# Six of eight output blocks transposed by VectorE and by transfers within SBUF, and the gate row summed in float32r

## The chip, the cores and the metric

The kernel runs on one core of one Trainium2 chip. A core has five engines that run side by side: TensorE (PE in the profile, with its weight loads apart as PEld), VectorE (DVE), ScalarE (ACT), GpSimd (POOL) and SyncE (SP, which here only issues transfers). The metric is the device time of one execution in microseconds (us), the median of several runs; less is better.

## The reference

One decoder layer: an adaLN-modulated RMSNorm, gated linear attention in chunks, a gated output projection and a final RMSNorm, on 1024 positions of width 1024, all in float32. Cut to what matters here:

```
mod = silu(c) @ ada_w + ada_b                      # shift, scale, gate: 1024 each
h   = rmsnorm(x, norm_g) * (1 + scale) + shift
q, k, v, g_lr, r = split(h @ w_in)
o   = gla(q, k, v, g_lr)                           # 4 heads, 1024 positions x 1024 values
o   = rmsnorm(o, gla_norm_g) * silu(r)
x   = x + gate * (o @ w_out)
out = rmsnorm(x, final_g)
```

Two parts of it are touched: `o` must be transposed so that its values lie on the partitions before `o @ w_out`, and `gate`, a row of 1024 sums, must stand on all 128 partitions before it is multiplied into `w_out`.

## The kernel before

The kernel does a float32 product as three float32r products: each operand is split into a high part (ScalarE copies it to float32r) and a low part (VectorE or GpSimd subtracts the high part), and `PAIRS` multiplies high with high, high with low and low with high. So each operand of a product passes through ScalarE and VectorE once.

The program is written in the order of PE's work, but issued in another: the class `Program` records every operation, and `schedule` plays them through with a table of costs (`cost`, `LAT`), in which each engine takes, of its operations that are ready, the one with the earliest latest start. What comes out is one fixed order for each engine; on the chip every engine works off its own list strictly in that order and waits at an instruction whose inputs aren't there. SP's transfers are issued from one such list too; each takes one of eight completion counters in turn, so that it waits for the transfer eight places ahead of it to have landed.

The main part is 32 steps `s`, 8 for each of four heads (`b = s // 8`) and one for each tile of 128 positions (`t = s % 8`). In a step PE forms the projection to v and r of one tile (24 products of 512 columns), and between them the hooks of `hooks(s)` run the linear attention of chunk `n = s - 4`: `e_head` to `e_kt` make the decays, `gla_at`, `gla_kv` and `gla_o` the products, and `gla_og` writes the gated, normed output of a chunk into `OG[n // 4]`, a tile of 128 positions by 4 by 256 values. So eight tiles `OG[b]` (b from 0 to 7) are filled one after the other, each over four steps. All of this goes through VectorE's list.

Then come 16 steps of the output projection, eight tiles for each half of the columns. `o_tr(t)` transposes the eight 128x128 blocks of one tile of positions on PE against the identity, into the PSUM banks `tr` and `md`, and splits them into `OT[t]` (tiles `hh` and `hl`), one step ahead of their use. `finish` adds the residual and takes the squares.

The gate row: `gate_acc` sums 16 pieces of `ada_w` times `silu(c)` into `GB` on VectorE, partition by partition, and `gate_bc(i)` adds up the 128 partitions of one half with a float32 product against a tile of ones on PE, whose result VectorE copies back into `GB`. `scale_piece` multiplies it into pieces of `w_out`.

In the trace the tile names stand without numbers: `ptr` and `pmd` are the PSUM banks `tr` and `md`, `ident` the identity, `qk` and `wa` the tiles that hold `OG` among others, `wg` is `GB`, `hh` and `hl` the split halves, `Sf` the attention state, `raw` pieces of a weight. Every operation is issued at one line, L217, so that rows are told apart by their tiles.

Of the kernel before, what the change touches and what calls it, by code (L numbers as in the profile page):

```python
# [8 lines left out]
F32R = mybir.dt.float32r  # L9
U8 = mybir.dt.uint8  # L10
AF = mybir.ActivationFunctionType
ALU = mybir.AluOpType
# [13 lines left out]
class Program:  # L26
# [7 lines left out]
    P = {"off": 8.0, "pad": 3.0}  # L34
# [29 lines left out]
    def cost(self, e, m, out, ins, kw):  # L64
        n = 1
        for d in out.shape[1:]:
            n *= d
        psum = any(a.space == bass.MemoryType.PSUM for a in ins + [out])
        if m == "dma_start":
            return n * out.shape[0] * 4 / 360e3  # L70
        if e == "pe":
            if m == "transpose":
                return 0.11
            k = 1 if ins[0].dtype == F32R else 4
            return 0.0135 + n * k / 2400 if n > 1 else 0.22
        if e == "act":
            return (0.05 if psum else 0.09) + n / 1200 + (0.2 if "accum_out" in kw else 0) + \
                (0.095 * sum(hasattr(kw.get(a, 0), "tensor") for a in ("scale", "bias")))
        if e == "dve":
            fast = m in ("tensor_copy", "tensor_scalar", "memset") and not psum  # L80
            return (0.13 if "scalar" in m else 0.068) + n * (0.52 if fast else 1.042) / 1000
        if m != "tensor_tensor":
            return 0.08 + n * 0.8 / 1000
        return 0.46 if kw.get("op") == ALU.pow else 0.11 + n * 2.1 / 1000
# [144 lines left out]
def gla_block(ctx, tc, x, c, ada_w, ada_b, norm_g, w_in, w_alpha, b_alpha, gn_g, w_out, final_g, out):  # L229
    nc = tc.nc  # L230
    prog = Program(nc)
    pe, act, dve, pool, sync = (prog.engine(e) for e in ("pe", "act", "dve", "pool", "sync"))
# [5 lines left out]
    def T(tag, shape, dt=F32):  # L238
        cnt[0] += 1
        return prog.tile(sb, tag, shape, dt, f"{tag}_{cnt[0]}")  # L240

    def P(tag, shape=(128, 512)):
        cnt[0] += 1
        return prog.tile(ps, "p" + tag, list(shape), F32, f"p{tag}_{cnt[0]}")

    def f(ap):
        return ap.bitcast(F32)
# [47 lines left out]
    ident = T("ident", [128, 128])  # L295
# [3 lines left out]
    ones = T("ones", [128, 128])  # L299
# [113 lines left out]
    def w_split(kt, c0=0, c1=384):  # L413
        if c0 == 0:
            WH[kt] = T(f"wa{2 * kt}", [128, D], F32R)
            WL[kt] = T(f"wa{2 * kt + 1}", [128, D], F32R)
        raw = WRAW[kt] if c0 == 0 else WRAW[kt, 3]
        hi, lo = (w[kt].rearrange("p (i c) -> p i c", i=2)[:, :, c0:c1] for w in (WH, WL))
        i = act.activation(hi, raw, AF.Copy)
        if c0 == 0 and kt > 1:  # L420
            prog.hold(i, HT[kt - 1])
        return dve.tensor_tensor(lo, raw, f(hi), op=ALU.subtract)
# [29 lines left out]
    def gate_w_load():  # L452
# [5 lines left out]
        for q0 in (0, 32, 96):  # L458
            sync.dma_start(war[q0:q0 + 16, :], w_alpha[0])

    def gate_w_conv():
        war = W["a"]
        act.activation(WA, war, AF.Copy)
        dve.tensor_tensor(WA[32:64, :], war[32:64, :], f(WA[32:64, :]), op=ALU.subtract)
# [46 lines left out]
    for kt in range(8):  # L511
# [5 lines left out]
        if kt == 0:  # L517
            for half in range(2):
                if half:
# [3 lines left out]
                    lo = w_split(1)  # L523
# [32 lines left out]
    gate_w_load()  # L556
    small_cols2()
    gate_w_conv()
    prog.first_loads = False
    for i, m in enumerate(M6):  # L560
# [25 lines left out]
    for i, m in enumerate((3, 7)):  # L586
        p = P(f"m{i}")
# [97 lines left out]
    OG, X, SHL, KD = {}, {}, {}, {}  # L685
# [128 lines left out]
    def og_tag(b):  # L814
        return f"wa{12 + b}" if b < 2 else f"qk{b // 2 - 1}{1 - b % 2}"
# [17 lines left out]
    GB = T("wg", [128, D])  # L833
# [11 lines left out]
    def gate_acc(i):  # L845
        kk, j = i // 2, i % 2
        g = GB[:, 512 * j:512 * j + 512]
        dve.scalar_tensor_tensor(g, GA[i], cact[:, kk:kk + 1], g, op0=ALU.mult, op1=ALU.add)

    def gate_bc(i):  # L850
        p = P("tr")
        pe.matmul(p, ones, GB[:, 512 * i:512 * i + 512], start=True, stop=True)
        dve.tensor_copy(GB[:, 512 * i:512 * i + 512], p)


    OT = {}

    def o_tr(t):
        oh = T(f"hh{t}", [128, 8, 128], F32R)
        ol = T(f"hl{t}", [128, 8, 128], F32R)  # L860
        OT[t] = (oh, ol)
        for g in range(2):
            p = P(("tr", "md")[g])
            for i in range(4):
                e = 4 * g + i
                src = OG[(e // 2) * 2 + t // 4][:, t % 4, 128 * (e % 2):128 * (e % 2) + 128]
                pe.transpose(p[:, 128 * i:128 * i + 128], src, ident)
            hi = oh[:, 4 * g:4 * g + 4, :].rearrange("p a b -> p (a b)")
            lo = ol[:, 4 * g:4 * g + 4, :].rearrange("p a b -> p (a b)")
            act.activation(hi, p, AF.Copy)  # L870
            dve.tensor_tensor(lo, p, f(hi), op=ALU.subtract)

    XRT = ["qk31", "G", "qk30", "wa7", "wa4", "wa5", "wa14", "wa8"]
    XR, FS = {}, {}
# [6 lines left out]
    def hooks(s):  # L881
        H = {}

        def at(k, fn, *a):
            H.setdefault(k, []).append((fn, a))

        n = s - LAG
        u = (s - 2) // 2
        b, t = s // 8, s % 8
        if t == 0 and 1 <= b < 6:  # L890
            for k in (6, 7):
                at(k - 6, conv_piece, b, k)
        if s % 4 == 1 and 5 <= s <= 33:
            at(4 if s < 33 else 0, silu, s // 4 - 1)
        if 0 <= u < 16:
            d = 0 if u > 3 else 2
            if s % 2 == 0:
                if d:
                    at(0, g_tr, u)
                at(d, e_head, u)  # L900
                at(3 + d // 2, e_scan, u)
                at(4 + d // 2, e_exp, u)
                at(6 + d // 2, e_mul, u)
            else:
                at(d // 2, e_split, u)
                at(3 + d // 2, e_kt, u)

        if 0 <= n - 1 < 32:
            at(0, gla_o, n - 1)
            at(6, gla_og, n - 1)  # L910
        if 0 <= n < 32:
            at(2, gla_at, n)
            at(5, gla_kv, n)
        if b < 5:
            x45, x67 = (f"qk{b}1", "wa6") if b < 4 else ("wa10", "wa11")
            if t == (2 if b >= 3 else 5):
                for k in range(4):
                    at(5, load_piece, b + 1, k)
            if (b, t) == (4, 4) or b < 4 and t == (2 if b == 3 else 5):
                for k in (6, 7):  # L920
                    at(5 if b < 4 else 0, load_piece, b + 1, k, x67)
            if t == 6:
                for k in (4, 5):
                    at(0, load_piece, b + 1, k, x45)
            if t == 7:
                for k in range(6):
                    at(k + 2, conv_piece, b + 1, k)
            if b >= 3:
                if 3 <= t < 6:
                    at(2, scale_piece, b + 1, (0, 2, 6)[t - 3])  # L930
                    at(5, scale_piece, b + 1, (1, 3, 7)[t - 3])
                if t == 6:
                    at(5, scale_piece, b + 1, 4)
                if t == 7:
                    at(0, scale_piece, b + 1, 5)
        if s < 5:
            for i in range(4):
                if s > 0:
                    at(i, gate_acc, 4 * (s - 1) + i)
                if s < 4:  # L940
                    at(4, gate_load, 4 * s + i)
            if s == 0:
                at(0, gate_init)
        if s == 5:
            at(0, gate_bc, 0)
        if s == 7:
            at(0, gate_bc, 1)
        if s >= 31 and s < 39:
            at(4 if s == 31 else 1, o_tr, s - 31)
        if s >= 32 and s < 40:  # L950
            at(4, load_xr, s - 32)
        return H
# [5 lines left out]
    for s in range(32):  # L958
        H = hooks(s)
        t = s % 8  # L960
        p = P(VB[s % 2])
# [6 lines left out]
        for kt in range(8):  # L968
            w = WP[s // 8, kt] if s >= 8 else WG[kt]
            for o, c0, c1 in groups:  # L970
                for j, (hi, wi) in enumerate(PAIRS):
                    h = (HH, HL)[hi][kt]
                    pe.matmul(o, h[:, 128 * t:128 * t + 128], w[:, wi, c0:c1],
                              start=(kt == 0 and j == 0), stop=(kt == 7 and j == 2))
# [7 lines left out]
    fg = None  # L982
    for s in range(32, 48):
        H = hooks(s)
        a, t = (s - 32) // 8, s % 8
        if a == 0:
# [8 lines left out]
        for i, (c0, c1) in enumerate(parts):  # L995
            p = P(VB[s % 2] if s < 47 else ("m0", "m1")[i])[:, 0:c1 - c0]
            for kt in range(8):
                w = WP[4 + a, kt]
                mm_o = OT[t]
                for j, (oi, wi) in enumerate(PAIRS):  # L1000
                    pe.matmul(p, mm_o[oi][:, kt, :], w[:, wi, c0:c1],
                              start=(kt == 0 and j == 0), stop=(kt == 7 and j == 2))
# [15 lines left out]
        if a == 1:  # L1018
            r = fss[:, 3:4]
# [32 lines left out]
```

## Time and profile before

| what | value |
|---|---|
| median of 3 runs | 453.7 us (453.37 to 455.35) |
| the profiled execution, its own time | 455.46 us |
| its span, first to last instruction | 453.7 us |
| PE busy | 440.6 us (97%) |
| VectorE busy | 313.4 us (69%) |
| ScalarE busy | 245.9 us (54%) |
| GpSimd busy | 127.8 us (28%) |
| granted clock, mean | 0.995 |

The profile is one execution on the chip. Busy is the time in which an engine had an instruction in work; matmuls are pipelined, so a matmul's own duration is longer than the distance to the next one, and it is the distance that counts for PE. An idle time is put down to what ended it. The chain of waits follows back from the last instruction what released each piece of work.

### The profile page before, as it was taken

Reading aid. Unit: us, or ns where it says so; the run is one execution under the profiler, and the core shown is the slowest. Engines: PE = TensorE matmul, PEld = TensorE weight load, DVE = VectorE, ACT = ScalarE, POOL = GpSimd, SP = SyncE. Lnnn points to the kernel's source line nnn. Section 1 sums busy time; section 2 is a strip of 40 time slices with the busy share of each in tenths; the row PEclk is TensorE's granted clock in tenths of the full one; section 3 lists DMA queues with packets and bytes.
Section 4 is the critical chain, followed back from the end, with each engine's and each line's share of the span. In section 5 each row is a group of like instructions: output and inputs, shape, how many; then the busy total and the mean of one; then the engine's idle time right before and its main releaser. Section 6 shows DMA issues by size and latency. Waiting matters only on the chain.

```text
span 453.7 us, 6865 instructions
## 1 busy us (share of the span) xinstructions
PE 440.6 (97%) x2426; PEld 377.8 (83%) x2426; DVE 313.4 (69%) x704; ACT 245.9 (54%) x564; POOL 127.8 (28%) x147
## 2 busy tenths in 40 slices
PE   8799999999999999999999999999999999999994
PEld 8687778888999998888888888878888888888883
DVE  2698856165216889987797877998789976464433
ACT  4675869110136667658668486685859641351111
POOL 3100201020002326442373524726256420040001
PEclk9999999999999999999999999999999999999998
DMA  8999752068200103100140001300014525002222
GB/s 270 351 310 305 249 119 60 25 189 266 56 1 0 48 12 93 38 0 12 36 117 24 0 12 36 117 24 1 1 47 147 190 95 172 1 1 92 92 94 92
DMA packets 40063, 43.09 MB, mean 95 GB/s; under 512 B 3847, under 2 KB 32685, under 8 KB 40030
## 3 DMA queue, kind: packets, MB, share of 16 engines
q1 hardware_dynamic: 39982, 42.65, 29.9%
q8 instruction: 19, 0.31, 0.3%
q14 instruction: 14, 0.11, 0.1%
q10 hardware_dynamic: 48, 0.01, 0.0%
HBM read 38.46 MB, written 4.19 MB: 94 GB/s over the span
## 4 chain that ended last, share of the span: by engine, by line
PE 73%; DVE 13%; DMA 6%; ACT 3%; issue 3%; SPq 1%; POOL 0%; POOLq 0%; DVEq 0%; ACTq 0%
PE pm L217 65%; DVE wa L217 7%; PE pmd L217 5%; DMA qk<-in_ada_w 4%; PE ptr L217 3%; DVE Sf L217 2%; DMA raw<-in_gla_w_in 1%; SPq L217 1%; ACT wa L217 1%; DVE x L217 1%; DVE v L217 1%; DVE raw L217 1%; DVE ATf L217 1%; ACT hl L217 0%; DVE rs L217 0%
## 5 line engine op out<-in xcount | busy, mean ns | idle before, releaser
L217 PE MATMUL pm<-x,hh 128*128 128x512 f32 (+2 forms) x424 | 121.9, 370 | 0.0
L217 PE MATMUL pm<-wa,hh 128*128 128x512 f32 (+2 forms) x424 | 120.6, 368 | 0.0
L217 PEld LDWEIGHTS pm<-wa,hh 128*128 128x128 f32 x424 | 73.5, 188 | 10.5
L217 PEld LDWEIGHTS pm<-x,hh 128*128 128x128 f32 x424 | 71.8, 189 | 9.0 <-issue 1.0
L217 PE MATMUL pm<-wa,hl 128*128 128x512 f32 (+2 forms) x212 | 77.3, 365 | 0.0
L217 PE MATMUL pm<-x,hl 128*128 128x512 f32 (+2 forms) x212 | 77.1, 364 | 0.0
L217 ACT ACTIVATE wa<-wa 128x256 f32<-128x256 f32 (+4 forms) x126 | 59.7, 496 | 21.6 <-DVE wa L217 16.4
L217 PE MATMUL pm<-hh,wa 128*128 128x512 f32 (+1 forms) x236 | 62.1, 386 | 1.0 <-ACT hh L217 1.0
L217 PEld LDWEIGHTS pm<-hh,wa 128*128 128x128 f32 x236 | 41.7, 188 | 9.2 <-ACT hh L217 2.0
L217 POOL TENSOR_TENSOR wa<-wa,wa 128x896 fp32r<-128x896 f32 (+1 forms) x22 | 43.0, 1956 | 14.0 <-ACT wa L217 14.0
L217 PEld LDWEIGHTS pm<-wa,hl 128*128 128x128 f32 x212 | 39.8, 188 | 6.7
L217 PEld LDWEIGHTS pm<-x,hl 128*128 128x128 f32 x212 | 39.8, 188 | 6.3
L217 PE MATMUL pm<-wa,wa 128*128 128x256 f32 (+1 forms) x208 | 38.5, 281 | 0.1
L217 POOL TENSOR_TENSOR Shl<-Sf,Shl 128x256 fp32r<-128x256 f32 x28 | 23.0, 821 | 47.4 <-ACT Shl L217 47.4
L217 PEld LDWEIGHTS pm<-wa,wa 128*128 128x128 f32 x208 | 31.7, 189 | 4.6 <-DVE wa L217 1.1
L217 POOL TENSOR_TENSOR ors<-oss,mh 128x1 f32<-128x1 f32 x32 | 19.7, 615 | 52.0 <-DVE oss L217 52.0
L217 ACT ACTIVATE qk<-pm 128x256 f32<-128x256 f32 (+1 forms) x31 | 12.9, 424 | 39.3 <-PE pm L217 30.7
L217 PE MATMUL pm<-hl,wa 128*128 128x512 f32 (+1 forms) x118 | 32.9, 382 | 0.0
L217 DVE TENSOR_TENSOR wa<-pm,wa 128x256 fp32r<-128x256 f32 (+2 forms) x37 | 17.9, 483 | 17.7 <-PE pm L217 11.3
L217 DVE TENSOR_TENSOR wa<-wa 128x256 f32<-128x256 f32 (+1 forms) x48 | 24.1, 525 | 8.1 <-ACT wa L217 7.9
L217 POOL TENSOR_TENSOR D<-wa 128x256 f32<-128x256 f32 x16 | 11.7, 732 | 62.5 <-DVE wa L217 58.8
L217 ACT ACTIVATE pm<-wa 128x512 f32<-128x512 f32 (+1 forms) x11 | 6.2, 561 | 38.1 <-DVE wa L217 30.9
(175 smaller groups left out, 766.7 us busy)
## 6 DMA issues: line engine op xcount, KB each, us to landing
qk<-in_ada_w SPq DMA_DIRECT2D x32, 256.0 KB, 5.8
raw<-in_gla_w_in SPq DMA_DIRECT2D x48, 128.0 KB, 2.2
raw<-in_ada_w SPq DMA_DIRECT2D x16, 256.0 KB, 3.4
raw<-in_gla_w_in SPq DMA_DIRECT2D x8, 384.0 KB, 5.7
qk<-in_x SPq DMA_DIRECT2D x6, 512.0 KB, 5.2
wa<-in_x SPq DMA_DIRECT2D x5, 512.0 KB, 4.1
x<-in_x SPq DMA_DIRECT2D x4, 512.0 KB, 3.4
raw<-in_gla_w_out SPq DMA_DIRECT2D x8, 256.0 KB, 3.7
```

The costliest lines, as they stand in the source:

```text
L217: getattr(self.eng[o["e"]], o["m"])(*o["call"][0], **o["call"][1])
```

## The change

Of the eight blocks `OG[b]`, those with b from 0 to 5 (heads 0 to 2) no longer go through PE. `o_blocks(b)`, hooked in the step in which such a block gets full, has VectorE transpose it in squares of 32 by 32 (four instructions of 128x256) into a tile `oy`, of which there is one, and SP move the 16 groups of squares within SBUF to where they belong, by 16 transfers of 32 partitions with 8 runs of 128 bytes each, into `O2[b]`. `o_tr(t)` then transposes only the two blocks of head 3 on PE, into one bank, and splits four pieces of 256 columns, three of them out of `O2` in SBUF, where it split two of 512 columns out of PSUM.

`gate_bc` multiplies with ones in float32r: `gate_split` first splits a half of `GB` into high and low on ScalarE and GpSimd, into the tile `wa6`, and PE does two float32r products where it did one float32 product. The tile of ones in float32r is one more VectorE instruction at the start. The table of costs gets a slower rate for transfers whose source is in SBUF. The order of all engines is worked out anew by the same rules.

```
--- before.py
+++ after.py
@@ -67,7 +67,7 @@
             n *= d
         psum = any(a.space == bass.MemoryType.PSUM for a in ins + [out])
         if m == "dma_start":
-            return n * out.shape[0] * 4 / 360e3
+            return n * out.shape[0] * 4 / (76e3 if ins[0].tensor.name in self.acc else 360e3)
         if e == "pe":
             if m == "transpose":
                 return 0.11
@@ -458,7 +458,10 @@
         for q0 in (0, 32, 96):
             sync.dma_start(war[q0:q0 + 16, :], w_alpha[0])
 
+    onesr = T("onesr", [128, 128], F32R)
+
     def gate_w_conv():
+        dve.tensor_copy(onesr, ones)
         war = W["a"]
         act.activation(WA, war, AF.Copy)
         dve.tensor_tensor(WA[32:64, :], war[32:64, :], f(WA[32:64, :]), op=ALU.subtract)
@@ -847,28 +850,51 @@
         g = GB[:, 512 * j:512 * j + 512]
         dve.scalar_tensor_tensor(g, GA[i], cact[:, kk:kk + 1], g, op0=ALU.mult, op1=ALU.add)
 
+    GS = {}
+
+    def gate_split(i):
+        if i == 0:
+            GS[0] = T("wa6", [128, 2, 512], F32R)
+        g = GB[:, 512 * i:512 * i + 512]
+        act.activation(GS[0][:, 0, :], g, AF.Copy)
+        pool.tensor_tensor(GS[0][:, 1, :], g, f(GS[0][:, 0, :]), op=ALU.subtract)
+
     def gate_bc(i):
         p = P("tr")
-        pe.matmul(p, ones, GB[:, 512 * i:512 * i + 512], start=True, stop=True)
+        for j in range(2):
+            pe.matmul(p, onesr, GS[0][:, j, :], start=j == 0, stop=j == 1)
         dve.tensor_copy(GB[:, 512 * i:512 * i + 512], p)
 
 
     OT = {}
+
+    def o_blocks(b):
+
+        y = T("oy", [128, 4, 8, 32])
+        for i in range(4):
+            dve.transpose(y[:, i].rearrange("p e i -> p (e i)"), OG[b][:, i, :])
+        O2[b] = T(og_tag(b), [128, 4, 2, 128])
+        yv = y.rearrange("p t (g c) i -> p t g c i", c=4)
+        for c in range(4):
+            for r in range(4):
+                sync.dma_start(O2[b][32 * c:32 * c + 32, :, :, 32 * r:32 * r + 32],
+                               yv[32 * r:32 * r + 32, :, :, c, :])
+
+    O2 = {}
 
     def o_tr(t):
         oh = T(f"hh{t}", [128, 8, 128], F32R)
         ol = T(f"hl{t}", [128, 8, 128], F32R)
         OT[t] = (oh, ol)
-        for g in range(2):
-            p = P(("tr", "md")[g])
-            for i in range(4):
-                e = 4 * g + i
-                src = OG[(e // 2) * 2 + t // 4][:, t % 4, 128 * (e % 2):128 * (e % 2) + 128]
-                pe.transpose(p[:, 128 * i:128 * i + 128], src, ident)
-            hi = oh[:, 4 * g:4 * g + 4, :].rearrange("p a b -> p (a b)")
-            lo = ol[:, 4 * g:4 * g + 4, :].rearrange("p a b -> p (a b)")
-            act.activation(hi, p, AF.Copy)
-            dve.tensor_tensor(lo, p, f(hi), op=ALU.subtract)
+        p = P(("tr", "md")[t % 2])
+        for i in range(2):
+            pe.transpose(p[:, 128 * i:128 * i + 128], OG[6 + t // 4][:, t % 4, 128 * i:128 * i + 128], ident)
+        for g in range(4):
+            hi = oh[:, 2 * g:2 * g + 2, :].rearrange("p a b -> p (a b)")
+            lo = ol[:, 2 * g:2 * g + 2, :].rearrange("p a b -> p (a b)")
+            src = O2[2 * g + t // 4][:, t % 4].rearrange("p a b -> p (a b)") if g < 3 else p[:, 0:256]
+            act.activation(hi, src, AF.Copy)
+            dve.tensor_tensor(lo, src, f(hi), op=ALU.subtract)
 
     XRT = ["qk31", "G", "qk30", "wa7", "wa4", "wa5", "wa14", "wa8"]
     XR, FS = {}, {}
@@ -941,10 +967,14 @@
                     at(4, gate_load, 4 * s + i)
             if s == 0:
                 at(0, gate_init)
+        if s == 4:
+            at(4, gate_split, 0)
         if s == 5:
             at(0, gate_bc, 0)
-        if s == 7:
-            at(0, gate_bc, 1)
+            at(0, gate_split, 1)
+            at(4, gate_bc, 1)
+        if s % 4 == 0 and 8 <= s <= 28:
+            at(7, o_blocks, s // 4 - 2)
         if s >= 31 and s < 39:
             at(4 if s == 31 else 1, o_tr, s - 31)
         if s >= 32 and s < 40:
```

What this moves is shown at three places. First PE's list in the output projection's first half, where a tile of positions is transposed between the products of a step; before:

```order
L217 MATMUL pm_545_608<-x_491_554,hh_532_595 128x512 x2
L217 MATMUL pm_545_608<-x_491_554,hl_533_596 128x512
L217 MATMUL ptr_612<-ident_72,wa_261_324 128x128 x2
L217 MATMUL ptr_612<-ident_72,qk_334_397 128x128 x2
L217 MATMUL pmd_613<-ident_72,qk_400_463 128x128 x2
L217 MATMUL pmd_613<-ident_72,qk_471_534 128x128 x2
L217 MATMUL pm_545_608<-x_492_555,hh_532_595 128x512 x2
```

and with the change, at the same place of the program:

```order
L217 MATMUL pm_555_618<-x_505_568,hh_543_606 128x512 x2
L217 MATMUL pm_555_618<-x_505_568,hl_544_607 128x512
L217 MATMUL ptr_622<-ident_72,qk_485_548 128x128 x2
L217 MATMUL pm_555_618<-x_506_569,hh_543_606 128x512 x2
L217 MATMUL pm_555_618<-x_506_569,hl_544_607 128x512
```

Four rows of two transposes became one row of two; the products around them stand as they did.

Second, VectorE's list around the first square transposes of block 2 (`oy`), in the second head's steps; before:

```order
L217 SCALAR_TENSOR_TENSOR qk_309_372<-pm_336_399,ors_285,qk_309_372 128x256
L217 SCALAR_TENSOR_TENSOR Sf_218_281<-Sf_219_282,dec_283,pm_339_402 128x256
L217 TENSOR_TENSOR wa_216_279<-pm_335_398,wa_216_279 128x256
L217 TENSOR_SCALAR wa_208_271<-ptr_410,cols_20_83 128x256
L217 TENSOR_SCALAR oss_284<-oss_284 128x1
L217 TENSOR_TENSOR wa_208_271<-wa_208_271 128x256
L217 COPY_PREDICATED ATf_206_269<-mask_267,pm_350_413 64x128
```

and with the change:

```order
L217 SCALAR_TENSOR_TENSOR qk_313_376<-pm_342_405,ors_286,qk_313_376 128x256
L217 SCALAR_TENSOR_TENSOR Sf_219_282<-Sf_220_283,dec_284,pm_345_408 128x256
L217 TENSOR_TENSOR wa_217_280<-pm_341_404,wa_217_280 128x256
L217 TENSOR_SCALAR wa_209_272<-ptr_416,cols_20_83 128x256
L217 TENSOR_SCALAR oss_285<-oss_285 128x1
L217 STREAM_TRANSPOSE oy_444<-qk_313_376 128x256
L217 TENSOR_TENSOR wa_209_272<-wa_209_272 128x256
L217 COPY_PREDICATED ATf_207_270<-mask_268,pm_356_419 64x128
```

The transpose into `oy` stands between the instructions of one chunk's output and those of the next unit's decays, and waits there until the 16 transfers of block 1 have read `oy`. The last transpose of block 1 stands 22 rows ahead of it:

```order
L217 SCALAR_TENSOR_TENSOR wa_263_326<-pm_333_396,ors_286,wa_263_326 128x256
L217 COPY Sf_220_283<-pm_336_399 128x256
L217 STREAM_TRANSPOSE oy_401<-wa_263_326 128x256
L217 TENSOR_TENSOR wa_209_272<-wa_209_272 128x256
L217 SCALAR_TENSOR_TENSOR wa_209_272<-rs_267,wa_209_272 128x256
```

Third, SP's list from the second head's weights on; before:

```order
L217 DMA raw_342_405<-in_gla_w_in 128x256 x2
L217 DMA raw_344_407<-in_gla_w_in 128x256 x2
L217 DMA wa_345_408<-in_gla_w_in 128x256 x4
L217 DMA qk_349_412<-in_gla_w_in 128x256 x4
L217 DMA raw_407_470<-in_gla_w_in 128x256 x2
L217 DMA raw_408_471<-in_gla_w_in 128x256 x2
L217 DMA raw_409_472<-in_gla_w_in 128x256 x2
```

and with the change:

```order
L217 DMA raw_349_412<-in_gla_w_in 128x256 x2
L217 DMA raw_350_413<-in_gla_w_in 128x256 x2
L217 DMA wa_351_414<-in_gla_w_in 128x256 x4
L217 DMA wa_312_375<-oy_374 32x8x32 x16
L217 DMA wa_339_402<-oy_401 32x8x32 x16
L217 DMA qk_355_418<-in_gla_w_in 128x256 x4
L217 DMA raw_417_480<-in_gla_w_in 128x256 x2
L217 DMA raw_418_481<-in_gla_w_in 128x256 x2
L217 DMA raw_419_482<-in_gla_w_in 128x256 x2
```

The 32 transfers of blocks 0 and 1 stand between the weights of one head and those of the next, and the weights behind them wait for VectorE's last transpose of block 1.

## Rows read from the trace of the kernel before

**Rows 1.** The page's busy times: us, share of the span, instructions.

```profile
PE 440.6 (97%) x2426; PEld 377.8 (83%) x2426; DVE 313.4 (69%) x704; ACT 245.9 (54%) x564; POOL 127.8 (28%) x147
```

**Rows 2.** What PE waited for, whole span: us in total, times, longest.

```profile
PE pmd L217 <- DVE D L217: 0.4, 1, 0.4
PE ptr L217 <- DVE wa L217: 0.3, 1, 0.3
```

**Rows 3.** Stretches: length; PE, PEld, DVE, ACT, POOL busy (count); clock; DMA share, GB/s.

```profile
146.00:176.00 30.00, 29.57 (x227) 27.47 (x226) 25.56 (x57) 20.04 (x51) 12.80 (x13) 1.00 0.16 44
176.00:206.00 30.00, 30.00 (x158) 25.44 (x159) 26.41 (x61) 19.07 (x47) 11.99 (x13) 1.00 0.10 29
206.00:236.00 30.00, 30.00 (x157) 25.27 (x156) 25.57 (x57) 20.55 (x53) 14.88 (x15) 1.00 0.20 54
236.00:266.00 30.00, 30.00 (x156) 24.95 (x155) 21.71 (x63) 21.80 (x51) 11.66 (x13) 1.00 0.07 19
266.00:281.00 15.00, 15.00 (x79) 12.64 (x78) 11.68 (x33) 9.48 (x30) 6.05 (x7) 1.00 0.13 36
281.00:304.00 23.00, 22.59 (x121) 19.00 (x120) 22.72 (x44) 16.67 (x39) 11.21 (x10) 1.00 0.22 70
...
342.00:372.00 30.00, 30.00 (x173) 25.74 (x172) 28.02 (x61) 20.29 (x48) 13.45 (x13) 1.00 0.41 137
372.00:397.00 25.00, 25.00 (x131) 21.04 (x130) 13.18 (x26) 6.80 (x16) 1.09 (x2) 1.00 0.32 106
```

**Rows 4.** The chain of waits: start us, us, what.

```profile
88.48 0.91 PE pm L217 x4
...
371.85 0.44 PE ptr L217 x4
```

**Rows 5.** PE in order of time at the first gate product: start, us, what.

```profile
150.44 1.02 PE L217 MATMUL ptr<-wg,ones 128*128 128x512 f32 x2
150.89 0.81 PE L217 MATMUL pm<-x,hh 128*128 128x272 f32 x2
151.54 0.29 PE L217 MATMUL pm<-x,hl 128*128 128x272 f32 x1
```

**Rows 6.** Groups of instructions by shape: count | busy us, mean ns | idle before.

```profile
L217 DVE TENSOR_TENSOR wa<-ATf,wa 128x128 fp32r<-128x128 f32 x32 | 17.8, 555 | 0.3
...
L217 DVE TENSOR_TENSOR_SCAN wa<-rs,wa 128x256 f32<-128x256 f32 x16 | 12.9, 806 | 0.3
...
L217 DVE TENSOR_TENSOR hl<-ptr,hh 128x512 fp32r<-128x512 f32 x8 | 5.5, 686 | 1.2 <-ACT hh L217 1.1
...
L217 DVE COPY Sf<-pm 128x256 f32<-128x256 f32 x4 | 1.7, 424 | 0.7 <-PE pm L217 0.7
...
L217 DVE TENSOR_TENSOR hl<-Shl,hh 128x256 fp32r<-128x256 f32 x2 | 0.9, 426 | 0.3 <-ACT Shl L217 0.3
```

**Rows 7.** SP in order of time, transfers merged: start, us, what.

```profile
154.88 1.75 SPq L217 DMA_DIRECT2D qk<-in_gla_w_in  x4
```

**Rows 8.** Transfers by line: count, KB each, median us from issue to landing.

```profile
x<-in_gla_w_alpha SPq DMA_DIRECT2D x3, 32.0 KB, 2.1
```

**Rows 9.** One stretch, columns as in rows 3, in which 64-byte runs land.

```profile
64.30:65.30 1.00, 0.77 (x4) 0.43 (x3) 0.48 (x2) 0.93 (x2) 0.20 (x1) 1.00 0.92 99
```

**Rows 10.** VectorE in order of time, four places of the heads' steps.

```profile
156.00 2.24 DVE L217 TENSOR_TENSOR wa<-ATf,wa 128x128 fp32r<-128x128 f32 x1
...
208.55 0.42 DVE L217 COPY Sf<-pm 128x256 f32<-128x256 f32 x1
...
219.74 0.42 DVE L217 TENSOR_TENSOR wa<-wa 128x256 f32<-128x256 f32 x1 [0.60 <-ACT wa L217]
...
295.45 2.73 DVE L217 SCALAR_TENSOR_TENSOR raw<-raw,cols,wg 128x512 f32<-128x512 f32 x4
```

**Rows 11.** GpSimd in order of time, beside the first of those.

```profile
155.97 2.12 POOL L217 TENSOR_TENSOR wa<-wa,wa 128x896 fp32r<-128x896 f32 x1 [1.93 <-ACT wa L217]
```

## The prediction, made before the changed kernel ran

> **What bounds the kernel now.** The page's busy times come first: PE is busy for 440.6 of 453.7 us, VectorE for 69%, ScalarE for 54% [rows 1]. Then the list of what PE waited for: after the first 90 us it holds two waits that matter, 0.3 and 0.4 us [rows 2]. So from there on PE works through its list almost without a gap, and what is taken off that list shortens the run, as long as nobody who feeds PE is late. Who could be late is read from the stretches [rows 3]: VectorE is busy for 25.6 of 30 us from 146, for 22.7 of 23 from 281 (there the wait of 0.4 for `D` falls) and for 28.0 of 30 from 342, while PE stands at 30.0 of 30 there. In the other stretches VectorE has 3 to 8 us of idle time. The changed part of PE's list is the output projection from 342 on, and the two gate products near 150.
>
> **What PE loses.** In the chain four transposes take 0.44 us [rows 4], so 0.11 each, placed between products and hidden by nothing. Of 8 x 8 = 64 in `o_tr`, 16 stay: 48 x 0.11 = 5.3 us. The gate's float32 product and two products of 272 columns behind it fill the time from 150.44 to 151.54, 1.10 us [rows 5]. A float32r product of 512 columns takes 0.91 / 4 = 0.23 us [rows 4], the two of 272 columns so 0.24; the float32 product costs 0.86. Two float32r products cost 0.46, which saves 0.40 on each half, 0.8 us together. PE's list gets shorter by 6.1 us.
>
> **What the others get.** VectorE: 24 square transposes of 128x256. The trace has none. The nearest row is a copy of 128x256 with 0.42 us [rows 6]; from below I bound it by half a 512-wide instruction, 0.34, from above by the scan over 128x256, 0.81 [rows 6]. I take 0.42, since a transpose too reads one operand once: 10.1 us in all (8.2 to 19.4), spread over the heads' steps. The low halves: 32 of 0.43 where there were 16 of 0.69 [rows 6], +2.7 us. The one cast of the ones falls into the start, where VectorE waits for the first loads. ScalarE gets 32 copies of 256 columns for 16 of 512 and has 9.7 us idle in the fullest of these stretches, GpSimd two subtractions [rows 3]: both nothing.
>
> Twenty-four of the new low halves read both operands from SBUF, where the old ones read one from PSUM. What that can cost is in two rows: an instruction of 128x128 with two SBUF operands took 2.24 us at 156.00, while GpSimd ran one of 2.12 from 155.97 [rows 10, 11]. The mean of its group is 0.56, though twice as wide a one takes 0.43 unheld [rows 6], so that a hold costs at least 0.13 on average. About 15 of the 24 fall where GpSimd is busy (13.5 of 30 us from 342 on, 1.1 of 25 after 372 [rows 3]): 2.0 us. The Trainium skill has a rule for this in "SBUF — State Buffer", section "Who interferes with whom": a VectorE instruction with two SBUF operands and a GpSimd instruction that reads SBUF share one port pair under an exclusive lock, and one with a single SBUF operand stays out of it. The trace agrees for the first half (2.24 beside 2.12 us); by the second half the square transposes are never held, which no row here shows.
>
> SP gets 96 transfers. One costs 1.75 / 4 = 0.44 us to issue [rows 7], and one of 32 KB lands 2.1 us after it [rows 8]. With eight in flight the issue sets the pace: 16 x 0.44 + 2.1 = 9.1 us a block. The first transpose of the next block waits for that, as `oy` exists once. For block 2 the room is read from the order and the trace: the last transpose of block 1 stands behind the copy that ends at 208.97, the first of block 2 ahead of the instruction at 219.74 [rows 10]; less 0.42 that is 10.3 us. So it fits by 1.2 us, and with the same 22 rows between at blocks 3 and 4. The weights behind the transfers on SP start some 3 us later than the 213.84 or so of before and are used some 10 us after that: no cost. Short runs: a load in 64-byte runs (`gw`) filled 92% of the transfer engines at 99 GB/s [rows 9]; at that rate the 512 KB of a block need 5.3 us, less than the 7.0 of issuing. "DMA: Bandwidth & Descriptors" of the Trainium skill, section "Specifications", speaks against these 128-byte runs: under 512 bytes a transfer reads, modifies and writes. Counted as double traffic that would be an estimated 10.6 + 2.1 = 12.7 us a block, 2.4 more than there is room for at three places, and the sum between 449.4 (VectorE's idle time takes it) and 456.6 (PE waits for all of it); no run here shows it for a source in SBUF.
>
> **What PE gives back.** From 146 to 176 PE runs just behind VectorE. That PE would come 0.8 us earlier gains nothing if VectorE does not, and VectorE gets two transposes of block 0 there, 0.8. Between 0 (its 4.4 us of idle time take it) and 1.6 I take 0.8. From 281 to 304 three transposes come in and one scaling of a weight piece, 2.73 / 4 = 0.68 [rows 10], moves out: 3 x 0.42 - 0.68 = 0.6, on an engine that has 0.3 idle; bounds 0 and 3 x 0.81 = 2.4; I take 0.6. From 342 to 372 PE needs 5 tiles x 6 x 0.11 = 3.3 us less, 26.7; VectorE needs 28.0 + 5 x (4 x 0.43 - 2 x 0.69) + 2.0 for holds = 31.7. That does not fit, but four scalings (2.7) can wait for the 11.8 idle us that follow [rows 3], and the pieces out of SBUF can be split before their step. Bounds 0 and 5.0; I take 0.4, since the low halves of the first tiles are ready long before PE comes to them. Together 1.8.
>
> **The sum.** 6.1 - 1.8 = 4.3 us off the span of 453.7: 449.4. The profiled execution took 455.5 by its own time, 1.7 us more than its span; it would be 451.2. The median of the unprofiled runs happens to be of the span's size, 453.7, and the same 4.3 us make it **449.4 us**.
>
> **Rivals.**
> First, VectorE becomes the bound in the three full stretches. For it: 22.7 of 23 and 28.0 of 30. Against: PE hardly waits at these places now. With transposes of 0.62, midway between copy and scan, it costs 1.6 + (3 x 0.62 - 0.68 = 1.2) + (31.7 - 2.7 - 26.7 = 2.3) = 5.1, and the gain shrinks to 1.0: 452.7 us.
> Second, nothing is given back: VectorE's idle 3 to 8 us per stretch and the new order swallow all of it. 453.7 - 6.1 = 447.6 us. For it: only two waits of PE in 360 us; against it the 0.3 idle us from 281.
> Third, on the slow side: the transfers within SBUF overlap less than loads from outside, and VectorE stands before `oy` at blocks 2, 3 and 4 with everything of the linear attention queued behind it (decays, masks, state), for which PE waits next. One at a time they would need 16 x 2.1 = 33.6 us a block; two at a time, 16 x 1.05 + 2.1 = 18.9, 8.6 beyond the room. VectorE's idle time takes 4.4, 8.3 and 3.3 of it [rows 3], PE loses 4.2 + 0.3 + 5.3 = 9.8: 453.7 - 4.3 + 9.8 = 459.2 us. It begins to outweigh the gain when a wait passes 6.0 us, at 0.9 us a transfer. Against it: 0.44 us of issue and 2.1 to landing, both of which leave room.
>
> **How the numbers follow.** The forecast gets 0.57, the first rival 0.19, the second 0.14, the third 0.10. A measurement of this kernel can tell about 0.5% from no change, 2.3 us: faster is under 451.4, slower over 456.0. The forecast and the second rival are faster (0.71), of the first a quarter (0.05), the rest of it within the bound (0.14); of the third 0.09 is slower and 0.01 within: 0.76, 0.15, 0.09. The range from 446.9 to 453.8 holds forecast, second rival and nearly all of the first; it leaves out the third and 0.04 on either side. The forecast's own range is 447.8 to 451.2.
>
> **What the profile after would show.** PE's transposes against the identity in the output projection: 16, in pairs of 0.22 us, and the `wg,ones` product gone. The square transposes near 0.42 us. The transfers out of `oy` issued at about 0.44 us each, and VectorE waiting for them for under 1 us in all. PE's waits after 90 us growing from under 1 to about 2 to 3 us, behind VectorE near 175, 303 and 350. VectorE's busy time up by 12 to 18 us. Wrong it would be if PE waits over 5 us in total in the heads' steps, or if VectorE's wait for transfers is several us per block.

## The result and the profile after

The changed kernel takes 458.1 us (median of 5 runs, 457.9 to 459.8) against 454.2 of the kernel before (median of 5, 453.4 to 455.4): the ratio is 1.0094, 95% interval 1.0068 to 1.012. It is slower by about 4 us; the forecast was 449.4 us, in a range from 446.9 to 453.8.

The page's busy times of the changed kernel, as in [rows 1]:

```profile
PE 438.7 (96%) x2378; PEld 373.9 (82%) x2378; DVE 318.5 (70%) x745; ACT 246.8 (54%) x582; POOL 132.3 (29%) x149
```

PE has 48 instructions less and is still not done earlier: it stands. What PE waited for, as in [rows 2] (us in total, times, longest):

```profile
PE pm L217 <- DVE wa L217: 3.8, 4, 1.6
...
PE pmd L217 <- DVE D L217: 0.9, 2, 0.5
PE pm L217 <- DVE x L217: 0.8, 1, 0.8
PE ptr L217 <- DVE hl L217: 0.7, 1, 0.7
```

The first row is new: PE stands before the low part of a chunk's masked products (`wa<-ATf,wa`, the last thing `gla_at` makes), which VectorE brings late. So the next view is what VectorE waited for, the rows with a transfer:

```profile
DVE oy L217 <- DMA qk<-oy: 4.4, 2, 2.3
DVE oy L217 <- DMA wa<-oy: 3.2, 1, 3.2
...
DVE qk L217 <- DMA qk<-in_gla_w_out: 3.0, 1, 3.0
```

VectorE waits 7.6 us before `oy`, at three places, and 3.0 us for a piece of the output projection's weights. The same in order of time, VectorE's rows at these places (start, us, what, idle before and what ended it):

```profile
208.40 0.43 DVE L217 STREAM_TRANSPOSE oy<-wa 128x256 f32<-128x256 f32 x1
...
221.79 0.45 DVE L217 STREAM_TRANSPOSE oy<-qk 128x256 f32<-128x256 f32 x1 [3.15 <-DMA wa<-oy]
...
240.83 0.76 DVE L217 STREAM_TRANSPOSE oy<-qk 128x256 f32<-128x256 f32 x2
...
253.64 0.45 DVE L217 STREAM_TRANSPOSE oy<-qk 128x256 f32<-128x256 f32 x1 [2.14 <-DMA qk<-oy]
...
268.55 0.43 DVE L217 STREAM_TRANSPOSE oy<-qk 128x256 f32<-128x256 f32 x1
...
281.07 0.45 DVE L217 STREAM_TRANSPOSE oy<-qk 128x256 f32<-128x256 f32 x1 [2.27 <-DMA qk<-oy]
...
339.77 1.42 DVE L217 SCALAR_TENSOR_TENSOR qk<-qk,cols,wg 128x512 f32<-128x512 f32 x2 [2.96 <-DMA qk<-in_gla_w_out]
```

These are the first transposes of blocks 2, 3 and 4, each behind the last one of the block before. And SP, as in [rows 7] (transfers in a row merged, start of the first to end of the last):

```profile
208.90 11.26 SPq L217 DMA_DIRECT2D wa<-oy  x16
...
241.62 10.40 SPq L217 DMA_DIRECT2D qk<-oy  x16
...
269.05 10.39 SPq L217 DMA_DIRECT2D qk<-oy  x16
...
300.89 35.34 SPq L217 DMA_DIRECT2D qk<-oy  x32
336.33 1.02 SPq L217 DMA_DIRECT2D qk<-in_gla_w_out  x2
```

Sixteen transfers keep SP for 10.40 us, 0.65 each. Block 3 shows the sum: last transpose of block 2 done at 240.83 + 0.76 = 241.59, SP done at 252.02, the last transfer landed and the next transpose begun at 253.64. That is 12.05 us, of which 9.9 went to VectorE's other work (and what that waits for) and 2.14 to standing before `oy`. Block 4 likewise (12.1, 9.8); block 2 took 13.0 against 9.8, as SP lost 0.9 more. The last two rows are the other wait. SP's row for the same two weight pieces in the kernel before:

```profile
327.89 0.80 SPq L217 DMA_DIRECT2D qk<-in_gla_w_out  x2
```

Now they come up at 336.33. The row of 32 transfers holds block 4, done at 311.3, and block 5:

```profile
325.83 10.40 SPq L217 DMA_DIRECT2D qk<-oy  x16
```

So the weights wait for block 5's sixteen alone. Of the 8.4 us a part is only that everything runs late by then; E1 below tells the two apart.

Three of the stretches of [rows 3] (columns as there):

```profile
206.00:236.00 30.00, 28.02 (x143) 23.09 (x142) 23.49 (x56) 18.98 (x51) 13.99 (x14) 1.00 0.29 66
...
281.00:304.00 23.00, 21.44 (x113) 17.89 (x112) 22.55 (x48) 15.69 (x36) 10.20 (x10) 1.00 0.31 96
342.00:372.00 30.00, 28.34 (x146) 22.71 (x145) 29.60 (x68) 28.33 (x78) 14.46 (x13) 1.00 0.35 118
```

PE stands for 2.0, 1.6 and 1.7 us where it stood for 0.0, 0.4 and 0.0. In the first of them VectorE does less than before (23.5 for 25.6 us): it is late, not full. The granted clock is 1.00 in these stretches as it was before, so none of this is the clock.

Where the time goes along PE's list is told by the start of one and the same product in two traces. The table gives how much later than in the kernel before a product starts, all set to 0 at 146.8 us (the columns are times in the kernel before; worked out from the traces). What lies ahead of 146.8 us is left out: it differs from trace to trace, by 2.1 us even between the kernel before and E11, which changes nothing there, so the medians of the runs need not differ by just what the table says.

| kernel | 154.7 | 193.4 | 257.4 | 295.5 | 334.5 | 355.1 | 401.1 |
|---|---|---|---|---|---|---|---|
| changed | -0.5 | +0.1 | +3.4 | +5.2 | +5.3 | +6.7 | +3.3 |
| E1 two `oy` | -0.5 | +0.1 | 0.0 | -0.1 | 0.0 | +1.7 | -1.6 |
| E5 two loads by ScalarE | -0.5 | +0.1 | +3.5 | +5.2 | +5.4 | +4.1 | +0.7 |
| E6 both | -0.5 | +0.1 | -0.1 | -0.2 | -0.1 | -1.3 | -4.7 |
| E2 repriced | -0.5 | +0.1 | -0.1 | -0.2 | -0.8 | -1.2 | -4.8 |
| E12 repriced, two loads by ScalarE | -0.5 | +0.1 | -0.1 | -0.2 | -0.9 | -2.2 | -5.5 |
| E4 gate alone | -0.5 | -0.4 | -0.4 | -0.4 | -0.4 | -0.4 | -0.4 |
| E10 half the transfers by ScalarE | -0.5 | +3.4 | +6.0 | +7.7 | +9.5 | +8.2 | +4.9 |

The changed kernel loses 3.3 us behind the first two waits for `oy` and 1.8 behind the third, together 5.1, and 1.4 net at the late weights (the saving on two tiles' transposes falls into the same stretch); from 376 us on it gains 0.64 us with every tile that has its six transposes less.

### The profile page after: what moved, and what is told of

Same layout as the page of the kernel before. It is cut to its first block, busy times and chain, and to the rows that moved or that the text cites. A ratio compares the mean times of both kernels' runs of the same rounds, so it can differ in the third digit from the quotient of the medians.

```text
span 457.2 us, 6953 instructions
## 1 busy us (share of the span) xinstructions
PE 438.7 (96%) x2378; PEld 373.9 (82%) x2378; DVE 318.5 (70%) x745; ACT 246.8 (54%) x582; POOL 132.3 (29%) x149
## 4 chain that ended last, share of the span: by engine, by line
PE 64%; DVE 19%; SPq 5%; ACT 4%; issue 3%; DMA 3%; POOL 1%; POOLq 0%; DVEq 0%; ACTq 0%
PE pm L217 56%; DVE wa L217 10%; PE pmd L217 5%; SPq L217 5%; PE ptr L217 3%; DVE x L217 1%; DVE Sf L217 1%; DMA qk<-in_ada_w 1%; DVE ATf L217 1%; DVE qk L217 1%; ACT L216 1%; ACT wa L217 1%; DVE oy L217 1%; DMA qk<-in_gla_w_out 1%; POOL D L217 1%
## 5 line engine op out<-in xcount | busy, mean ns | idle before, releaser
L217 PE MATMUL pm<-hh,wa 128*128 128x512 f32 (+1 forms) x236 | 64.0, 397 | 0.0
L217 PEld LDWEIGHTS pm<-hh,wa 128*128 128x128 f32 x236 | 43.7, 200 | 7.6 <-ACT hh L217 0.2
L217 POOL TENSOR_TENSOR wa<-wa,wa 128x896 fp32r<-128x896 f32 (+1 forms) x22 | 44.8, 2037 | 10.6 <-ACT wa L217 10.5
L217 POOL TENSOR_TENSOR ors<-oss,mh 128x1 f32<-128x1 f32 x32 | 18.7, 584 | 54.6 <-DVE oss L217 54.6
L217 PEld LDWEIGHTS pm<-hl,wa 128*128 128x128 f32 x118 | 22.5, 198 | 4.3
```

Source lines behind the costliest of these rows:

```text
L217: getattr(self.eng[o["e"]], o["m"])(*o["call"][0], **o["call"][1])
```

## The experiments

Theory 1: the transfers' pace. A transfer within SBUF keeps SP longer than forecast, so VectorE stands before `oy`, and PE behind it. Theory 2: VectorE's added work alone is too much. Theory 3: SP's longer list makes the loads behind it late. Each time is given as a ratio to the kernel before, run on the same chip. In every run the planner lays out the order of all engines anew, so an edit can also move instructions that it doesn't touch.

**E1 and E2: the waits for `oy`.** E1 gives `oy` two buffers (and halves a scratch area for transfers, to make room):

```
-        y = T("oy", [128, 4, 8, 32])
+        y = T(f"oy{b % 2}", [128, 4, 8, 32])
...
-    nc = bacc.Bacc(..., dynamic_dma_scratch_size=4096)
+    nc = bacc.Bacc(..., dynamic_dma_scratch_size=2048)
```

> Two buffers `oy` in turn, so that the transposes of a block no longer wait for the transfers of the block before. Theory 1 (a transfer within SBUF takes 0.61 us of SP, 16 take 11.8 us with the landing, and with one `oy` VectorE stands at blocks 2, 3 and 4): VectorE's waits for transfers out of `oy` (7.6 us in the changed kernel) fall under 1 us, PE's loss between 193 and 300 us (5.2 us) goes, and the time comes to about 453 us; the late weights of the output projection stay late. Theory 2 (VectorE's added work, about 13 us, is what PE waits for, and the waits on `oy` only take up idle time): 457 to 458 us. Theory 3 (SP's list is the harm: the loads behind the transfers come late, the one before the output projection by 8 us): 457 us, since the list is as long as before.

E2 changes one number in the planner's table, and so the order in which VectorE and SP get their work, but none of the work:

```
-                ring = max(ring, t) + 0.475
+                sb = o["call"][0][1].tensor.name in self.acc
+                ring = max(ring, t) + (0.65 if sb else 0.475)
```

> The planner counts 0.65 us of SP for a transfer out of SBUF in place of 0.475; the work is the same. Theory 1: it then puts other VectorE work ahead of the transposes of blocks 2, 3 and 4, VectorE waits under 3 us in all for `oy`, and the time is 453 to 455 us. Theory 2: the work is the same, so the time is 457 to 459 us. Theory 3: the planner can now put the weights of the output projection ahead of transfers; 455 to 457 us.

E1: 454.2 us, ratio 0.9991 (0.9979 to 1.0004). Of the waits for `oy` none is left, and PE's loss up to 295 us is gone with them (table). The order moved too (the first transpose of block 1 stands at 190.58 us, where it stood at 197.85), so E1 alone does not tell the second buffer from the new order. The wait for the weights stays, SP's and VectorE's rows in E1:

```profile
331.70 1.02 SPq L217 DMA_DIRECT2D qk<-in_gla_w_out  x2
```

```profile
335.00 1.41 DVE L217 SCALAR_TENSOR_TENSOR qk<-qk,cols,wg 128x512 f32<-128x512 f32 x2 [3.29 <-DMA qk<-in_gla_w_out]
```

PE is not late here (0.0 at 334.5 us in the table), and the weights still start 3.8 us later than before: that is their own lateness.

E2: 449.6 us, ratio 0.9910 (0.9892 to 0.9928), a larger gain than any theory gave it. VectorE's and SP's rows in E2 (at L218, since the kernel is a line longer):

```profile
208.85 0.43 DVE L218 STREAM_TRANSPOSE oy<-wa 128x256 f32<-128x256 f32 x1
...
226.73 0.43 DVE L218 STREAM_TRANSPOSE oy<-qk 128x256 f32<-128x256 f32 x1
```

```profile
209.35 10.93 SPq L218 DMA_DIRECT2D wa<-oy  x16
...
331.15 1.02 SPq L218 DMA_DIRECT2D qk<-in_gla_w_out  x2
```

The transfers are as slow as ever, but the transpose of block 2 now comes 17.9 us behind that of block 1, with other work between, and stands no more. The weights come late still (331.15), but the scaling that needs them is set behind other work too and waits for nothing. Theory 2 is out: the same instructions, in another order, give back 8.5 us.

**E3: the transfers' work taken away.**

```
-        for c in range(4):
-            for r in range(4):
-                sync.dma_start(O2[b][32 * c:32 * c + 32, :, :, 32 * r:32 * r + 32], ...)
+        sync.dma_start(O2[b].rearrange("p t g i -> p (t g i)"), y.rearrange("p t e i -> p (t e i)"))
```

> Each block's 16 transfers become one straight copy of 512 KB from `oy` to the block's new place, so the 32x32 blocks stay where they are on the partitions: this leaves out the exchange between partitions, and the output is not the reference's. VectorE's, ScalarE's and PE's work stay as they are. Theory 1 and theory 3: SP issues 6 transfers for 96, no wait for `oy`, no late weights, and the prediction's other terms are left: 449 to 451 us. Theory 2: VectorE's work is unchanged, so 456 us or more.

Measured 451.2 us, ratio 0.9936 (0.9918 to 0.9953). VectorE's list of waits holds no transfer out of `oy` and no piece of the output projection's weights any more. The time is 0.2 us above what theories 1 and 3 gave, which E3 cannot tell apart, and far from theory 2's 456.

**E4: the gate alone** (the kernel before with `gate_split` and the new `gate_bc`).

> The kernel before with the gate row's sum as two float32r products, and nothing else of the change. All theories: PE's list is shorter by 0.8 us near 150 us; the prediction has the gate's gain kept, 452.5 to 453.2 us against 453.7; if PE stands behind VectorE from 146 to 176, nothing of it is left and the time is that of before.

Measured 453.8 us, ratio 1.0003 (0.9990 to 1.0017): no difference that can be told, where 0.5 to 1.2 us were expected. In the trace PE gains 0.5 us at the first half's product and keeps 0.4; the second half's adds nothing.

**E5, E6 and the control E11: the late weights.** One edit, put on the changed kernel (E5), on E1 (E6) and on the kernel before (E11):

```
-            sync.dma_start(r, woutk[kt, :, 512 * (b - 4):512 * (b - 4) + 512])
+            q = act if slot == "qk31" else sync
+            q.dma_start(r, woutk[kt, :, 512 * (b - 4):512 * (b - 4) + 512])
```

> The changed kernel, with the two loads of the output projection's pieces 4 and 5 (tile qk31), which stand on SP behind 32 transfers, issued by ScalarE instead. Of the 7.6 us by which the changed kernel's matmuls ran behind those of the repriced kernel at the end, 5.2 came at the waits for `oy` and the rest, 2.3, between 336 and 372 us. If the late weights are that rest: 458.1 - 2.3 = 455.8 us, and VectorE's wait of 3.0 us at 337 is gone. If VectorE's and ScalarE's work in this stretch is the rest: 458 us.

> Two buffers `oy` and the two loads issued by ScalarE. If the waits for `oy` and the late weights are the whole of what went wrong: 454.2 - 2.3 = about 451.5 to 452, near the repriced kernel's 449.6 and no more than 2 us over it. If VectorE's added work between 342 and 372 us costs more than the prediction's 0.4 us: 454 us.

> A control: the kernel before with the two loads into qk31 issued by ScalarE, and nothing else. VectorE waited 0.5 us for them and PE did not wait behind it, so the time is that of before, 453.3 to 454 us; were it 2 us shorter, the gain of the changed kernel with this edit would be no property of the change.

E5: 454.8 us, ratio 1.0006 (0.9993 to 1.0019); the wait for the weights is gone, the three for `oy` are as they were, and from 334.5 to 355.1 us PE gains 1.3 where the changed kernel lost 1.4. What VectorE's other instructions take there is the same in both (the longest low half 2.30 and 2.29 us), so the gain is that of the weights. E6: 449.9 us, ratio 0.9887 (0.9872 to 0.9902): of these waits 0.2 us is left, and 4.7 us are gained. E11: 453.9 us, ratio 0.9999 (0.9989 to 1.0009), so the edit does nothing without the change. The two causes add up: 5.1 us for `oy`, 2.6 for the weights (between 334.5 and 355.1 us the changed kernel loses 1.4 and E6 gains 1.2), 7.7 of the 8.0 that lie between the two in the table.

**E7 and E9: what the transfer's price hangs on.** Both keep 16 transfers of 32 KB a block and copy straight, E7 32 partitions in runs of 1 KB, E9 128 partitions in runs of 256 bytes:

```
+                sync.dma_start(O2[b][32 * c:32 * c + 32, r].rearrange("p g i -> p (g i)"),
+                               y[32 * c:32 * c + 32, r].rearrange("p e i -> p (e i)"))
```

```
+        for c in range(8):
+            for r in range(2):
+                sync.dma_start(ov[:, c, 64 * r:64 * r + 64], yv[:, c, 64 * r:64 * r + 64])
```

> Sixteen transfers of 32 KB a block as in the changed kernel, but each copies 32 partitions straight in runs of 1 KB instead of 256 runs of 128 bytes (the exchange between partitions is left out, and the output is not the reference's). If the 0.61 us that SP takes for a transfer come from the number of runs, a transfer takes about 0.47 (what one straight copy of 512 KB took), 16 and the landing 9.4 us, which the prediction's room of 10.3 us holds: VectorE waits under 1 us for `oy` and the time is about 450 us. If 0.61 is the price of any transfer from SBUF to SBUF on 32 partitions: waits as in the changed kernel, 458 us.

> Sixteen transfers of 32 KB a block as in the changed kernel, but each copies all 128 partitions straight in runs of 256 bytes (the exchange between partitions is left out, and the output is not the reference's). If SP's price hangs on the 32 partitions: about 0.44 to 0.47 us a transfer, 16 and the landing 9.0 to 9.4 us, inside the 9.8 us that the changed kernel's VectorE had between its transposes, wait for `oy` under 0.5 us, the weights less late: 451 to 453 us. If it is the price of any transfer from SBUF to SBUF of this size: 0.59 to 0.61 us, and 456 to 458 us.

E7: 456.1 us, ratio 1.0027 (1.0010 to 1.0044). E9: 456.7 us, ratio 1.0062 (1.0044 to 1.0079). The transfers' rows (ns, shortest, median, longest), first the changed kernel's, then E7's, then E9's:

```profile
L217 SPq DMA_DIRECT2D qk<-oy x64: 586/609/620, 241.6 to 335.6; - x64
```

```profile
L217 SPq DMA_DIRECT2D qk<-oy x64: 507/589/599, 240.7 to 333.6; - x64
```

```profile
L217 SPq DMA_DIRECT2D qk<-oy x64: 465/599/611, 240.8 to 334.0; - x64
```

Eight times longer runs take 0.02 us off, four times as many partitions 0.01: both expectations that laid the price to the shape are wrong. Only the first of a series is cheaper (the shortest value), and that one hangs on the shape: the 512 KB copies of E3, one by one over 128 partitions, took 0.47 as the first in E9. The size of 32 KB does not explain the price either, as three loads of 32 KB out of HBM in the changed kernel show:

```profile
L217 SPq DMA_DIRECT2D x<-in_gla_w_alpha x3: 416/418/522, 62.6 to 63.6; - x3
```

The waits for `oy` stay, 5.9 us in E7 and 6.8 in E9. In all three the median from issue to landing is 1.9 us.

**E8 and E12: both remedies at once.** E8 is E1 with E2's number, E12 is E2 with E5's edit.

> Two buffers `oy` and the planner's 0.65 us for a transfer out of SBUF, both. If the repriced kernel already has VectorE free of waits for transfers, the second buffer adds nothing: 449 to 450 us. If moving the transposes back still costs something, 448 us.

> The repriced kernel (0.65 us) with the two loads issued by ScalarE. In the repriced kernel VectorE did not wait for these weights any more, since the scaling of them was set later: so the edit adds nothing, 449 to 450 us. If they still cost something there, 448 us.

E8: 450.5 us, ratio 0.9905 (0.9889 to 0.9920): the second buffer adds nothing to E2. E12: 448.8 us (448.6 to 449.2), ratio 0.9887 (0.9874 to 0.9899), the shortest of all, and it leaves out nothing of the reference. That the weights have no more part in E2 did not come true to the last: against E2 it gains 0.7 us in the table, though by their ratios the two can hardly be told apart.

**E10: half of the transfers issued by ScalarE.**

```
-                sync.dma_start(O2[b]...
+                (act if r % 2 else sync).dma_start(O2[b]...
```

> The changed kernel with half of the transfers (r = 1 and 3) issued by ScalarE. Eight on SP take 8 x 0.61 + 1.9 = 6.8 us a block, inside the 9.8 us: no wait for `oy`, and the weights behind them less late. If ScalarE pays 0.61 us for each of its 48 (4.9 us a block) and its idle 45% hides that: 450 to 451.5 us. If ScalarE's activations behind the issues hold up VectorE and PE: 454 us or more.

Measured 458.5 us, ratio 1.0095 (1.0081 to 1.0109). VectorE waits for no transfer out of `oy` any more, and PE waits more than ever. PE's wait, then ScalarE (its queue is ACTq) and VectorE at block 0, all of E10:

```profile
PE pmd L217 <- DVE D L217: 8.4, 6, 2.5
```

```profile
182.32 4.14 ACTq L217 DMA_DIRECT2D wa<-oy  x6
186.50 0.42 ACT L217 ACTIVATE D<-D 128x256 f32<-128x256 f32 x1 [3.83 <-DMA wa<-oy]
```

```profile
186.95 0.43 DVE L217 TENSOR_TENSOR D<-D,qk 128x256 f32<-128x256 f32 x1 [2.77 <-ACT D L217]
```

Six issues stand in ScalarE's list ahead of an activation of the decays, 0.69 us each; VectorE waits for that, PE for VectorE. ScalarE's idle 46% is no room for them, since it lies elsewhere.

## Why the prediction was wrong, step by step

**The step that failed** is "16 x 0.44 + 2.1 = 9.1 us a block ... So it fits by 1.2 us". The room was read nearly right (10.3 us forecast, 9.8 found at three blocks), and so was the landing; the issue was not: 0.65 a transfer, 10.4 for sixteen, 12.05 in all. The 0.44 came from loads out of HBM [rows 7], and I took it as the price of a kind of transfer that no row showed, with no upper bound on it in the range; at 0.65 the same sum says at once that it does not fit, by 2.2 us at three blocks. E1, E2, E6 and E12 show it: take away the wait, by a second buffer or by order alone, and 5.1 us come back. The prediction's own sign of being wrong, a wait of several us a block, is what the trace shows.

**The step has a second half.** With 0.65 in its place the prediction would have found the waits and, by the reckoning of its own third rival, still lost nothing by them: it let VectorE's idle time take the first 4.4, 8.3 and 3.3 us of a wait [rows 3], and waits of 2.2 lie below all three. In fact the idle time took 2.5 of the 7.6 us, and PE lost the other 5.1. That idle time is mostly waiting for answers of PE and ScalarE, and a late VectorE makes those late too: in the stretch of blocks 2 and 3 (206 to 253.5 us before, 205.4 to 256.3 now) VectorE waited some 9 us for PE and ScalarE before and still some 6 now, with 5.3 us at `oy` beside them. A share of idle time is not slack. With the waits and the late weights (below) put in, the account closes: -4.3 as forecast, + 5.1 for `oy` + 2.6 for the weights is +3.4, and the table has +3.3 at 401.1.

**The weights behind the transfers** ("some 3 us later ... no cost") are the second part of the same mis-sized term. The prediction took one load, behind block 1, and not the last of the list, behind block 5's sixteen transfers. There "some 3 us later" is about right (3.8 in E1, where nothing else is late), but "no cost" is not: VectorE waits 3.0 us for them, and that costs 2.6 (E5, E6, E11).

**The third rival** named the place, and its 459.2 us came close by luck. Its price was wrong in both directions: it needed transfers of 1.05 us and waits of 8.6 us over the room, and said a wait begins to outweigh the gain at 6.0 us, since idle time takes the first 3 to 8. Waits of 3.15, 2.14 and 2.27 us, and the late weights, which it did not have, were enough.

**Right were** PE's saving in the transposes, 0.64 us a tile or 5.1 in all (5.3 forecast); the square transposes, 0.43 us (0.42); and ScalarE's copies, which cost nothing where the order is good (after 90 us PE waits for ScalarE nowhere in E2 and E6). The gate was forecast to gain 0.8 and to have it given back by 176 us; it gains 0.4 alone (E4) and nothing with block 0's transposes beside it (+0.1 at 193.4 us). Its second product stood at 166.9 us in the kernel before, not near 150. What PE gives back was right in its sum and not in its terms: near 300 us it gives back nothing (forecast 0.6; E6 stands at -0.1 at 257.4 and at -0.1 at 334.5), in the output projection 0.5 in E6 and 1.2 in E2 (forecast 0.4). So it is in part luck that E2 ends 4.75 us ahead in the table (forecast 4.3) and takes 449.6 us beside the forecast 449.4; it also has another order than the kernel that was forecast.

**VectorE's busy time** was to grow by 12 to 18 us and grew by 5.1. Rows of the changed kernel as in [rows 6] (count, busy us, mean ns):

```profile
L217 DVE TENSOR_TENSOR wa<-ATf,wa 128x128 fp32r<-128x128 f32 x32 | 13.9, 435 | 0.2
...
L217 DVE TENSOR_TENSOR hl<-qk,hh 128x256 fp32r<-128x256 f32 x16 | 8.7, 562 | 0.0
...
L217 DVE TENSOR_TENSOR hl<-wa,hh 128x256 fp32r<-128x256 f32 x8 | 4.9, 609 | 0.0
...
L217 DVE TENSOR_TENSOR hl<-ptr,hh 128x256 fp32r<-128x256 f32 x4 | 1.7, 422 | 0.1
```

The low halves out of SBUF take 0.56 and 0.61 in the mean where one out of PSUM takes 0.42: 16 x 0.14 + 8 x 0.19 = 3.7 us of holds, forecast 2.0. But the mean hides what happens (ns, shortest, median, longest):

```profile
L217 DVE TENSOR_TENSOR hl<-qk,hh x16: 410/416/2297, 348.4 to 388.0; 128x256 fp32r<-128x256 f32 x16
```

Twenty of the 24 take 0.41 to 0.42, and all of the 3.7 us falls on four, of 0.64, 0.87, 1.74 and 2.30 us, each of which began while GpSimd had a subtraction of 256 or 896 columns in work. With the transposes the added instructions cost 16.0 us (10.0, and 17.0 of low halves for 11.0), forecast 14.8. But the first row fell from 555 to 435 ns, 3.9 us in all, and with others like it 7.4 us went out of the old instructions: where VectorE's list shifts, others stand beside GpSimd's, and the sum of holds is not the old one plus the new. (The rest of the difference is that instructions overlap at their ends, which the busy time counts once.)

The short runs, which the prediction weighed as a danger, were none. Its estimate of 12.7 us a block came near the 12.05, for a wrong reason: with 1 KB runs (E7) a transfer takes 0.59 us and lands in 1.9 as with 128 bytes. The page of the Trainium skill that it rested on, "DMA: Bandwidth & Descriptors", says in its section "Why small descriptors are slow (HBM only)" that transfers from SBUF to SBUF do not have this penalty, and E7 agrees.

## What to carry to other kernels

A transfer within SBUF has its own price on the queue that issues it; before a buffer is reused behind sixteen of them, count pace and landing against the work that lies between, and follow the queue to the last load behind them. When a planner sets the order, its table is part of the kernel: here one number in it, 0.475 or 0.65 us, was the difference between 458 and 450 us with the same instructions. And an engine's idle time takes up a wait only where nobody's answer is late behind it, so price a new wait from 0 (idle time takes it) to all of it, at every place where it can occur.

## What the runs showed of the hardware

Back to back, a transfer of 32 KB from SBUF to SBUF kept SP for 0.59 to 0.61 us whatever its shape (32 or 128 partitions, runs of 128 bytes to 1 KB), while four loads of 128 partitions out of HBM kept it for 0.44 each [rows 7]; the first of a series cost 0.47 to 0.59. Three loads of 32 KB out of HBM took 0.52, 0.42 and 0.42, so the size is not the reason; nor is the number in flight, since already the second of a series took 0.58 to 0.61 within SBUF, and mostly 0.42 to 0.43 out of HBM. Of what the runs varied, only the place of the source is left; no run took the same shape from both places, and why one costs more is open. A load out of HBM right behind such a series took 0.54, the next one 0.43. From ScalarE's queue the same transfers took 0.62 us, and an activation behind them in its list waited.

All 24 square transposes took between 400 and 448 ns, with GpSimd busy beside 12 of them. This is the second half of the rule weighed in the prediction (the Trainium skill, "SBUF — State Buffer", section "Who interferes with whom"): an instruction with one operand in SBUF stays out of the lock, unless it runs in one of the faster modes that use both of VectorE's ports. The trace agrees.
